# Placing the gate's sum, the transposes of queries and keys, and the last steps of a filler tile in a one-core hybrid attention layer

## The chip, the cores and the metric

The kernel runs on one core of a Trainium2 chip, in fp32 accuracy. The metric is the device time of one execution in microseconds (us). Before the change three runs gave 1677.49, 1675.11 and 1676.13 us; the median is 1676.13 us. A difference of about 0.2% is what the measurement of this kernel can tell from none.

## The reference, cut to what matters

One layer (D = 1024, 1024 latent tokens, 256 context tokens) computes a gated linear attention (GLA, 4 heads) and a differential attention (8 heads) on the same normalised input, and merges them.

```python
for layer in range(DEPTH):                      # DEPTH = 1
    mod_x = silu(c) @ w_ada + b_ada             # shift, scale, gate g_x
    ...
    pl = project(modulate(x, sh_x, sc_x), w_in)
    pc = project(modulate(ctx, sh_c, sc_c), w_in)
    ...
    o_gla = bidir_gla(q, k, v, la_f, la_b, s_f, s_b)
    ...                                         # q1, q2, k1, k2: rms_norm * gain, rotary positions
    o_diff = diff_attention(q1, q2, [ck1, k1], [ck2, k2], [cv, dv], lam)
    # a = softmax(q1 k1 / 8) - lam * softmax(q2 k2 / 8), then a @ v
    a = rms_norm(o_gla) * gla_gain * silu(gla_gate)
    b = rms_norm(o_diff) * diff_gain * (1 - lam_init) * silu(diff_gate)
    y = sigmoid(m_gla) * (a @ w_br_gla) + sigmoid(m_diff) * (b @ w_br_diff)
    x = x + g_x * (y @ w_out)
```

## The kernel before, in words

**Arithmetic.** An fp32 product is made of three TensorE (PE) matmuls per step of 128 rows (`mm3`: high·high, low·high, high·low), because each operand is held as a high and a low part. The splitting is done on ScalarE (ACT), VectorE (DVE) and GpSimd (POOL).

**Who sets the order.** The program is not written in the order in which it runs. Some dozens of Python generators each describe a job. `Driver.run` (L159) keeps a modelled time for every engine, takes the due generator with the lowest priority number, lets it issue instructions up to its next `yield`, and so writes one fixed list for every engine; the chip then only follows semaphores. The modelled time `now` is that of PE: a PE instruction is written at `now`, whether its operands are there on the chip or not. `yield At(t)` comes back up to 1 us before t (`AHEAD`), `yield AtPE(t)` not before PE's time has reached t. So `yield AtPE(e)` says "place what follows on PE where its operand `e` is ready by the model, and not earlier". If the model is too hopeful, PE waits on the chip.

**Stages.** (1) From 0 to about 500 us: the modulation, the normalised input, the projections, `job_gate`. (2) To about 910 us: GLA, interleaved with the projections of dk, dq and m. (3) About 910 to 1466 us: the differential attention. (4) To the end: the output products on PE.

**`job_gate` (L745)** makes the gate g_x: for each half `n`, DVE adds eight scaled rows of weights into `gb` (L764), PE sums over the partitions with a matmul of `ones` and `gb` into the PSUM tile `tp` (L773), and DVE adds the bias. L770 places the matmul.

**`post_qk` (up to L1363)** finishes one tile `p` of queries or keys: squares on ACT, gains, rotary products and sums on DVE, then on POOL the power of -1/2 and its product with the tile (L1343 to L1346); then PE transposes it in four pieces into `tp` (L1353), and it is split and stored. L1347 places the transposes. There are 36 such groups of four.

**Attention.** A unit is one head and 128 queries (64 units); two units make a pair. `att_scores` (L1784) computes for each unit two maps ("components") of 1280 scores in the PSUM tile `s5` (rows `s<-hk,aq`): eight matmuls of 512 columns and four of 256. DVE takes the maxima (`sm<-s`), ACT the exponentials (`e<-s,sm`), which free the bank for the next scores; DVE mixes both maps (`e<-e,sm,e`). `att_tr` (L1877) transposes the mixed map in groups of 4, 4 and 2 (L1897, rows `b<-ident,e`), each group is split (`att_split`: ACT's copy `ac<-b` with POOL's `at<-ac,at`, or ACT and DVE for the third group), and `att_av` (L1902) multiplies the pair with the values: 30 matmuls of 256 columns (rows `b<-at,vv`). `att_fin` follows with two transposes per unit (`b<-ident,b1k`). All these share two PSUM banks, `b1`.

**Filler.** `fill` has the lowest priority and gives PE independent matmuls: half tiles of 8 steps of 3 matmuls (rows `mb<-h,wt`, 128x512) in one PSUM bank, `mb`. 12 tiles are for the m gates (kind 0: eviction by ACT, `ft<-mb`), 8 for the GLA branch (kind 1) and 8 for the other branch (kind 2). A kind 1 tile also loads its gate values. `half_tile` (L2070) comes back to the planner after every step of three, so that a tile can lie open across several scores, transposes and products; the next can begin only when the bank is evicted. What is not filled by the end of stage 3 is done at its end, in other banks.

Of the kernel before, what the change touches and what calls it, by code (L numbers as in the profile page):

```python
# [25 lines left out]
NK = D // P  # L26
# [202 lines left out]
class Hybrid:  # L229
# [515 lines left out]
    def job_gate(self):  # L745


        a = self.a
        yield from self.acq("gb")
        gb = self.t("gb", [P, 2, 512])  # L750
        for n in range(2):
            o = 2048 + n * 512
            for kk in range(NK // 2):
                yield from self.acq("raw")
                raw = self.t("raw", [P, 2, 512])
                self.dma(raw, a["w_ada"][0][kk * 256:(kk + 1) * 256, o:o + 512].rearrange("(k p) c -> p k c", p=P))
                yield self.d.when(raw)
                for j in range(2):
                    k = 2 * kk + j
                    c = self.col[:, k:k + 1]  # L760
                    if k == 0:
                        e = self.dve.tensor_scalar(gb[:, n], raw[:, j], c, None, ALU.mult)
                    else:
                        e = self.dve.scalar_tensor_tensor(gb[:, n], raw[:, j], c, gb[:, n], ALU.mult, ALU.add)  # L764
                    yield e
                self.rel("raw", e)
            yield from self.acq("p")
            bias = self.t("p", [P, 512])
            self.dma(bias, a["b_ada"][0:1, o:o + 512].to_broadcast([P, 512]))
            yield self.d.whenpe(gb)  # L770
            yield from self.acq("tp")
            pm = self.t("tp", [P, 512])
            e = self.mm(pm, self.ones, gb[:, n], True, True)  # L773
            yield e
            yield self.d.when(bias)
            e = self.dve.tensor_tensor(bias, pm, bias, ALU.add)
            self.rel("tp", e)
            yield e
            self.rel("p", self.pool.tensor_scalar(gb[:, n], bias, 0.5, 0.0, ALU.mult, ALU.add))
        self.store([(self.d_gb, gb)], ("gb", 1), ev=self.ev_gb)  # L780
# [531 lines left out]
    def post_qk(self, isk, c, i, pm):  # L1312

        nc = self.nc
        g8 = lambda ap: ap.unsqueeze(1).to_broadcast([P, 8, 64])
        pv = pm.rearrange("p (g e) -> p g e", e=64)
        if isk and (c, i) == (1, 9):
            self.rel("hc", self.d.now, 16)
        yield self.ev_rope[isk]
        yield from self.acq("p", 2)  # L1320
        sq = self.t("p", [P, 8, 64])
        self.act.activation(sq, pv, AF.Square)
        ss = self.t("sm", [P, 8])
        r = self.t("p", [P, 8, 64])
        if i >= 8:
            e = self.dve.tensor_tensor(r, pv, g8(self.gains[:, isk, 0]), ALU.mult)
        else:
            e = self.dve.tensor_tensor(r, pv, g8(self.rope[:, 0, i]), ALU.mult)
        yield self.d.when(sq)
        self.dve.tensor_reduce(ss, sq, AX.X, ALU.add)  # L1330
        if i < 8:
            rv = sq.rearrange("p g (a h e) -> p g a h e", a=2, h=2)
            xv = pv.rearrange("p g (a h e) -> p g a h e", a=2, h=2)
            sv = self.rope[:, 1, i].rearrange("p (a h e) -> p a h e", a=2, h=2)
            for hh in range(2):
                e = self.dve.tensor_tensor(rv[:, :, :, hh], xv[:, :, :, 1 - hh],
                                           sv[:, :, hh].unsqueeze(1).to_broadcast([P, 8, 2, 16]), ALU.mult)
            self.dve.tensor_tensor(r, r, sq, ALU.add)
            if (c, i) == (1, 7):
                self.rel("rope", self.d.when(r))  # L1340
        self.rel("mm", e)
        yield self.d.when(ss)
        self.pool.tensor_scalar(ss, ss, 1.0 / 64, EPS, ALU.mult, ALU.add)  # L1343
        self.pool.tensor_tensor(ss, ss, self.nhalf, ALU.pow)
        yield self.d.when(r)
        e = self.pool.tensor_tensor(r, r, ss.unsqueeze(2).to_broadcast([P, 8, 64]), ALU.mult)  # L1346
        yield AtPE(e)  # L1347
        yield from self.acq("tp")
        yield from self.acq("pl", 2)
        pt = self.t("tp", [P, 4, P])  # L1350
        rf = r.rearrange("p g e -> p (g e)")
        for j in range(4):
            e = self.tr(pt[:, j], rf[:, j * P:(j + 1) * P])  # L1353
        self.rel("p", e, 2)
        yield e
        hi = self.t("pl", [P, 4, P], F32R)
        lo = self.t("pl", [P, 4, P], F32R)
        e = yield from self.split(pt, hi, lo)
        self.rel("tp", e)
        o = self.tok(i) if isk else i * P  # L1360
        dst = [self.d_kT[j][c] if isk else self.d_qT[c][:, :, j] for j in range(2)]
        self.store([(dst[j][:, :, o:o + P].rearrange("h p t -> p h t"), x) for j, x in enumerate((hi, lo))],
                   ("pl", 2), ev=self.ev_st["dk" if isk else "dq", c, i])  # L1363
# [420 lines left out]
    def att_scores(self):  # L1784
# [4 lines left out]
        for hd in range(8):  # L1789
            for qt in range(8):  # L1790
                pr, qs = qt // 2, slice((qt % 2) * P, (qt % 2) * P + P)
                yield self.ev_k[hd]
                yield self.ev_q[hd, pr]
                K, Q = self.K[hd], self.Q[hd, pr]

                def score(po, comp, o, n):
                    bank = po.offset % (2 * T) // 512
                    for j in range(2):
                        e = self.mm(po, Q[comp][:, j, qs], K[comp][:, o:o + n], j == 0, j == 1)
                        self.banked(self.ins, "PE", bank)  # L1800
                    return e

                u = dict(hd=hd, qt=qt, E=[None, None], mt=self.t("sm", [P, 2]), mx=[self.t("sm", [P, 1]) for _ in range(2)],
                         z=self.t("sm", [P, 2]), left=2, ev=[Event() for _ in range(3)])

                for comp in range(2):
                    yield from self.acq(f"s{comp}")
                    pm = s5[:, 1536 * comp:1536 * comp + 1024]
                    for x, (o, n) in enumerate(self.MAIN[comp]):
                        e = score(pm[:, x * 512:(x + 1) * 512], comp, o, n)  # L1810
                        if x == 0:
                            yield AtPE(0)
                    d.spawn(self.att_max(u["ev"][comp], u["mx"][comp], pm, 3 * comp, 3 * comp + 1), On(e, "DVE"), prio=-3)
                    yield AtPE(0)
                    if comp == 0:
                        yield from self.acq("st")
                        pt = s5[:, 1024:1536].rearrange("p (c k) -> p c k", c=2)
                        for x in range(2):
                            e = score(pt[:, x], x, *self.TAIL[x])
                        d.spawn(self.att_max(u["ev"][2], u["mt"], pt, 2), On(e, "DVE"), prio=-3)  # L1820
                    elif qt == 7:
                        self.rel("kk", e, 2)
                    d.spawn(self.att_exp(u, comp, s5), On(e, "DVE"), prio=-3)
                    yield AtPE(0)
                if qt % 2 == 1:
                    self.rel("aq", e, 2)
                d.set(self.ev_u[8 * hd + qt])
# [49 lines left out]
    def att_tr(self):  # L1877

        d = self.d
        for hd in range(8):  # L1880
            for qt in range(8):
# [5 lines left out]
                for g, (k0, n) in enumerate(self.GROUPS):  # L1887
# [5 lines left out]
                    tb = "mc" if "psC" in self.pools else "b1"  # L1893
                    yield from self.acq(tb)
                    pt = self.t(tb, [P, n, P])
                    for j in range(n):
                        e = self.tr(pt[:, j], E[:, (k0 + j) * P:(k0 + j + 1) * P])  # L1897
                    d.spawn(self.att_split(g, pt, hi[:, :, x], lo[:, :, x], self.ev_aT[hd, qt, g], tb), On(e, "ACT"), prio=self.PS)
# [3 lines left out]
    def att_av(self):  # L1902
        d = self.d
        for hd in range(8):
            for pr in range(4):
# [8 lines left out]
                for g, (k0, n) in enumerate(self.GROUPS):  # L1914
                    hi, lo, tg = A[g]
                    for x in range(2):
                        yield self.ev_aT[hd, 2 * pr + x, g]
                    for j in range(n):
                        kt = k0 + j
                        e = self.mm3(po, VH[:, kt], VL[:, kt], hi[:, j].rearrange("p x t -> p (x t)"),  # L1920
# [10 lines left out]
    DT = (0, 4, 1, 5, 2, 6, 3, 7)  # L1931
    PO, FI = "b1", "mb"
    PACE = 1.3
    PT, PA = 1, 2
    PC = ()

# [82 lines left out]
    def fill(self):  # L2019
# [50 lines left out]
        def half_tile(n, half, rhs):  # L2070
# [10 lines left out]
                self.dma(mt, self.d_m[0][s][:, half * 512:(half + 1) * 512])  # L2081
            elif kind == 2:
                d.spawn(self.load_y(s, half), prio=-1)
            for k in range(NK):
                if kind:
                    yield rhs.ev[k, half]
                e = self.mm3(pm, hi[:, k], lo[:, k], rhs[0][k][half], rhs[1][k][half], k == 0, k == NK - 1)
                yield AtPE(0)
            if half == 1:
                self.rel("wt", e, 2)  # L2090
            if kind == 2:
                d.spawn(self.post_y(tg, s, half, pm), e, prio=-1)
            else:
                d.spawn(post(tg, kind, s, half, pm, mt), e, prio=self.PP)
            return e

        class Rhs(list):
            pass
# [396 lines left out]
```

## Time and profile before

| | |
|---|---|
| runs | 1677.49, 1675.11, 1676.13 us |
| profiled execution | 1676.87 us |
| its span, first to last instruction | 1675.2 us |
| mean granted TensorE clock | 0.998 |
| PE busy | 1634.8 us (98%) |
| DVE busy | 1166.3 us (70%) |
| ACT busy | 796.3 us (48%) |
| POOL busy | 606.4 us (36%) |
| PE busy in attention (910 to 1466 us) | 541.0 of 556 us |

How to read it: a matmul's busy time runs from its start to its modelled end, and neighbours overlap; so the start-to-start distance of matmuls, and not the mean busy time of one, tells what a matmul costs. In a timeline row the bracket at the end gives the idle time of the engine just before it and the instruction that ended it; `x12` means that twelve instructions of a kind were merged to a row. In a window row the columns after the stretch are its length, then the busy time and count of PE, PE's weight loads, DVE, ACT and POOL, the granted TensorE clock, the DMA share and GB/s. In a group row stand the busy time and the mean of one, then the idle time just before its members and who ended it.

### The profile page before, as it was taken

What the parts mean: (1) busy time and instruction counts of PE and PEld (TensorE: products, weight loads), DVE (VectorE), ACT (ScalarE), POOL (GpSimd) and SP (SyncE); (2) the same over time, 40 slices, a digit from 0 to 9 for tenths busy, and PEclk for the clock granted to TensorE, in tenths of its full rate; (3) what the DMA queues carried; (4) which work ended last, traced back from release to release, by engine and by line L of the source; (5) the groups of instructions that cost most, each with busy time, mean ns of one, the idle gap of its engine ahead of it and who ended that gap; (6) DMA issues with size and microseconds to landing.
All of it is one profiled execution on the core that took longest, in us unless ns stands there. A gap on an engine that the chain in (4) does not pass through costs nothing.

```text
span 1675.2 us, 24268 instructions
## 1 busy us (share of the span) xinstructions
PE 1634.8 (98%) x8389; PEld 1354.1 (81%) x8389; DVE 1166.3 (70%) x2019; ACT 796.3 (48%) x1640; POOL 606.4 (36%) x649
## 2 busy tenths in 40 slices
PE   7999999999999999999999999999999999999999
PEld 3688788888788888888878887888888888888887
DVE  4797853455578697687762878877887787438594
ACT  4766423343434535455441666665666556413141
POOL 1500200000156575464540544546565565700000
PEclk9999999999999999999999999999999999999999
DMA  8557947677573675646466244334336743277422
GB/s 304 175 204 259 326 163 248 230 276 276 201 251 120 187 218 174 186 137 177 123 187 162 68 122 129 106 107 133 114 107 196 247 126 108 65 255 250 158 78 76
DMA packets 248971, 294.44 MB, mean 176 GB/s; under 512 B 20712, under 2 KB 169104, under 8 KB 248848
## 3 DMA queue, kind: packets, MB, share of 16 engines
q1 hardware_dynamic: 248848, 292.90, 55.4%
q8 instruction: 66, 1.08, 0.3%
q14 instruction: 57, 0.47, 0.1%
HBM read 199.51 MB, written 93.32 MB: 175 GB/s over the span
## 4 chain that ended last, share of the span: by engine, by line
PE 43%; DVE 7%; ACT 3%; issue 2%; POOL 1%; DMA 1%; SPq 0%; ACTq 0%; DVEq 0%; POOLq 0%
PE mc L335 11%; PE mm L335 7%; PE mb L335 7%; PE s L335 6%; PE b L335 5%; DVE sm L197 4%; PE b L361 3%; ACT e L197 2%; DVE e L197 2%; PE go L335 1%; POOL at L197 1%; PE mz L335 1%; PE gs L335 1%; PE tp L361 1%; PE gt L335 1%
## 5 line engine op out<-in xcount | busy, mean ns | idle before, releaser
L335 PE MATMUL mm<-w,h 128*128 128x512 f32 x1260 | 319.1, 402 | 0.6 <-DVE w L197 0.4
L335 PEld LDWEIGHTS mm<-w,h 128*128 128x128 f32 x1260 | 231.9, 189 | 47.9 <-issue 1.0
L197 DVE TENSOR_REDUCE sm<-s 128x1 f32<-128x1024 f32 (+1 forms) x192 | 194.1, 1038 | 44.5 <-PE s L335 38.8
L335 PE MATMUL mb<-h,wt 128*128 128x512 f32 x744 | 202.0, 404 | 0.8 <-ACT ft L197 0.5
L197 ACT ACTIVATE e<-s,sm 128x1280 f32<-128x1280 f32 x128 | 170.1, 1333 | 60.8 <-DVE sm L197 50.0
L197 POOL TENSOR_TENSOR at<-ac,at 128x512 fp32r<-128x512 f32 x128 | 191.2, 1493 | 10.7
L197 POOL TENSOR_SCALAR at<-ac 128x512 fp32r<-128x512 f32 x128 | 101.3, 791 | 251.4 <-ACT ac L197 153.7
L335 PE MATMUL s<-hk,aq 128*128 128x512 f32 (+1 forms) x768 | 179.5, 366 | 6.1 <-ACT e L197 4.2
L335 PEld LDWEIGHTS mb<-h,wt 128*128 128x128 f32 x744 | 130.9, 189 | 24.4 <-ACT ft L197 2.2
L335 PEld LDWEIGHTS s<-hk,aq 128*128 128x128 f32 x768 | 120.5, 189 | 27.2 <-ACT e L197 11.7
L335 PE MATMUL mm<-h,w 128*128 128x512 f32 x576 | 137.6, 394 | 2.2 <-DVE h L197 1.1
L335 PE MATMUL mc<-h,wt 128*128 128x512 f32 x600 | 137.7, 390 | 0.0
L335 PE MATMUL b<-at,vv 128*128 128x256 f32 x960 | 131.3, 285 | 0.5 <-POOL at L197 0.3
L335 PEld LDWEIGHTS mc<-h,wt 128*128 128x128 f32 x600 | 112.1, 188 | 23.1
L335 PEld LDWEIGHTS mm<-h,w 128*128 128x128 f32 x576 | 106.9, 188 | 26.2 <-DVE h L197 1.6
L335 PEld LDWEIGHTS b<-at,vv 128*128 128x128 f32 x960 | 123.3, 190 | 5.7 <-POOL at L197 0.9
L197 DVE TENSOR_TENSOR w<-raw,w 128x512 fp32r<-128x512 f32 x120 | 92.6, 790 | 32.1 <-ACT w L197 30.9
L197 ACT ACTIVATE ac<-b 128x512 f32<-128x512 f32 x120 | 71.1, 601 | 90.9 <-PE b L361 84.2
L197 POOL TENSOR_TENSOR sm<-sm,nhalf 128x2 f32<-128x2 f32 (+2 forms) x94 | 102.3, 1089 | 26.0 <-DVE sm L197 20.8
L197 DVE SCALAR_TENSOR_TENSOR e<-e,sm,e 128x1280 f32<-128x1280 f32 x64 | 110.4, 1725 | 1.0
L197 ACT ACTIVATE w<-raw 128x512 fp32r<-128x512 f32 x120 | 72.5, 629 | 70.8 <-DVE raw L197 22.8
L197 POOL TENSOR_TENSOR p<-p,gdif 128x512 f32<-128x512 f32 x12 | 16.2, 1359 | 242.6 <-DMA d_dv<-pl 194.6
(283 smaller groups left out, 2914.2 us busy)
## 6 DMA issues: line engine op xcount, KB each, us to landing
raw<-in_w_in SPq DMA_DIRECT2D x63, 512.0 KB, 4.5
g<-d_s SPq DMA_DIRECT2D x32, 640.0 KB, 5.0
aq<-d_qT SPq DMA_DIRECT2D x128, 128.0 KB, 3.1
d_dv<-pl SPq DMA_DIRECT2D x40, 256.0 KB, 2.1
gv<-d_v SPq DMA_DIRECT2D x40, 256.0 KB, 3.1
d_kT<-pl SPq DMA_DIRECT2D x40, 256.0 KB, 2.9
hk<-d_kT SPq DMA_DIRECT2D x32, 320.0 KB, 4.9
vv<-d_dv SPq DMA_DIRECT2D x16, 640.0 KB, 5.7
```

Of the source, the lines that this page charges most:

```text
L197: self.ins = f(out, *args, **kw).ins
L335: self.ins = self.nc.tensor.matmul(out, lhsT, rhs, start=start, stop=stop, skip_group_check=more).ins
L361: self.nc.tensor.transpose(out, src, self.ident[:n, :n])
```

## The change

Three places move. The sums on each engine stay the same: 8077 PE instructions in the program, 2021 on DVE, 1408 on ACT, 654 on POOL and 962 on SP, before and now.

1. The gate's sum is placed 4 us of modelled time after `gb` is ready (it was 0).
2. The transposes of a query or key tile are placed 1.5 us after POOL's product is ready (it was 0).
3. A half tile of the filler that is open has its remaining steps written at once ("flushed") at three places, if there are few: one remaining step before the scores of each component, one before each group of transposes, and up to two (`FN`) before the first of the three groups of the values' products (`FG = (0,)`). Steps of kinds 1 and 2 are flushed only if their operands have landed by the model.

```diff
@@ job_gate
-            yield self.d.whenpe(gb)
+            yield AtPE(self.d.when(gb) + 4)
             yield from self.acq("tp")
             pm = self.t("tp", [P, 512])
             e = self.mm(pm, self.ones, gb[:, n], True, True)
@@ post_qk
         e = self.pool.tensor_tensor(r, r, ss.unsqueeze(2).to_broadcast([P, 8, 64]), ALU.mult)
-        yield AtPE(e)
+        yield AtPE(e + 1.5)
@@ att_scores
                     pm = s5[:, 1536 * comp:1536 * comp + 1024]
+                    if self.flush:
+                        self.flush(1)
                     for x, (o, n) in enumerate(self.MAIN[comp]):
@@ att_tr
                     pt = self.t(tb, [P, n, P])
+                    if self.flush:
+                        self.flush(1)
                     for j in range(n):
@@ att_av
                         yield self.ev_aT[hd, 2 * pr + x, g]
+                    if g in self.FG and self.flush:
+                        self.flush(self.FN)
                     for j in range(n):
@@ class
+    flush, FG, FN = None, (0,), 2
@@ half_tile
-            for k in range(NK):
-                if kind:
-                    yield rhs.ev[k, half]
-                e = self.mm3(pm, hi[:, k], lo[:, k], rhs[0][k][half], rhs[1][k][half], k == 0, k == NK - 1)
-                yield AtPE(0)
-            if half == 1:
-                self.rel("wt", e, 2)
-            if kind == 2:
-                d.spawn(self.post_y(tg, s, half, pm), e, prio=-1)
-            else:
-                d.spawn(post(tg, kind, s, half, pm, mt), e, prio=self.PP)
-            return e
+            x = [0, None]
+
+            def step():
+                k = x[0]
+                x[0] += 1
+                e = x[1] = self.mm3(pm, hi[:, k], lo[:, k], rhs[0][k][half], rhs[1][k][half], k == 0, k == NK - 1)
+                if k == NK - 1:
+                    self.flush = None
+                    if half == 1:
+                        self.rel("wt", e, 2)
+                    if kind == 2:
+                        d.spawn(self.post_y(tg, s, half, pm), e, prio=-1)
+                    else:
+                        d.spawn(post(tg, kind, s, half, pm, mt), e, prio=self.PP)
+
+            def flush(n):
+                if 0 < NK - x[0] <= n and not (kind and any(rhs.ev[k, half].t is None or rhs.ev[k, half].t > d.now for k in range(x[0], NK))):
+                    while x[0] < NK:
+                        step()
+
+            self.flush = flush
+            while x[0] < NK:
+                if kind:
+                    yield rhs.ev[x[0], half]
+                if x[0] < NK:
+                    step()
+                    yield AtPE(0)
+            return x[1]
```

**What moves on PE at the second gate sum.** In the rows, `mm` is a projection's PSUM tile, `w` its weights, `h` the activations, `tp` the sum's tile; numbers are buffers. Before, PE in the projections ahead of about 197 us:

```order
L335 MATMUL mm_1961<-w_1385,h_170_720 128x512
L335 MATMUL mm_1961<-w_1384,h_171_721 128x512
L335 MATMUL mm_1961<-w_1639,h_178_763 128x512
L335 MATMUL mm_1961<-w_1640,h_178_763 128x512
L335 MATMUL mm_1961<-w_1639,h_179_764 128x512
L335 MATMUL tp_1973<-gb_1135,ones 128x512
```

And now, at the same sum:

```order
L335 MATMUL mm_2015<-w_1384,h_171_721 128x512
L335 MATMUL mm_2014<-w_1635,h_178_763 128x512
L335 MATMUL mm_2014<-w_1636,h_178_763 128x512
L335 MATMUL mm_2014<-w_1635,h_179_764 128x512
L335 MATMUL tp_2034<-gb_1135,ones 128x512
L335 MATMUL mm_2015<-w_1635,h_178_763 128x512
```

The sum was PE's row 780 and is its row 807: 27 matmuls of 512 columns later; two projection tiles now run side by side around it. (The first sum goes from row 596 to row 611.)

**What moves on PE at the last but one transposes of queries.** `go` and `gs` are GLA's outputs and scores. Before:

```order
L335 MATMUL gs_8187<-gqr_8044,gkk_805_4255 128x64 x2
L335 MATMUL mm_8127<-h_140_598,w_8121 128x512
L335 MATMUL mm_8127<-h_141_599,w_8121 128x512
L335 MATMUL mm_8127<-h_140_598,w_8122 128x512
L361 MATMUL tp_8212<-ident,p_8131 128x128 x4
L335 MATMUL mm_8127<-h_146_613,w_8152 128x512
```

And now:

```order
L335 MATMUL mm_8145<-h_134_577,w_8017 128x512
L335 MATMUL go_8179<-gsf_7803,gqe_7906 128x256
L335 MATMUL go_8179<-gsb_7281,gqe_7909 128x256
L335 MATMUL go_8179<-gv_1569_7806,gsc_8141 128x256
L335 MATMUL go_8179<-gsf_7967,gqe_7906 128x256
L335 MATMUL go_8179<-gsb_7100,gqe_7909 128x256
L335 MATMUL go_8179<-gv_1569_7806,gsc_8141 128x256
L361 MATMUL tp_8186<-ident,p_8077 128x128 x4
L335 MATMUL mm_8145<-h_140_598,w_8052 128x512
```

Six steps of the next tile and GLA's six output matmuls, which stood behind the transposes, now stand ahead of them.

**What moves in a pair of units in the middle of the attention.** `s_1691_8515` is the tile of the scores, `b_...` a bank of transposes, `mb` the filler's bank. Before, PE between two groups of transposes of one map:

```order
L361 MATMUL b_2336_11437<-ident,e_2235_10986 128x128 x4
L335 MATMUL s_1691_8515<-hk_8182,aq_11157 128x512 x4
L335 MATMUL mb_11425<-h_181_766,wt_10679 128x512
L335 MATMUL mb_11425<-h_182_767,wt_10679 128x512
L335 MATMUL mb_11425<-h_181_766,wt_10680 128x512
L335 MATMUL s_1691_8515<-hk_8182,aq_11157 128x256 x2
L335 MATMUL s_1691_8515<-hk_8182,aq_11160 128x256 x2
L335 MATMUL s_1691_8515<-hk_8182,aq_11160 128x512 x4
L361 MATMUL b_2345_11476<-ident,e_2235_10986 128x128 x4
```

And now, at the same place:

```order
L361 MATMUL b_2334_11451<-ident,e_2252_11069 128x128 x4
L335 MATMUL mb_11422<-h_181_766,wt_10807 128x512
L335 MATMUL mb_11422<-h_182_767,wt_10807 128x512
L335 MATMUL mb_11422<-h_181_766,wt_10808 128x512
L335 MATMUL mb_11422<-h_187_792,wt_10807 128x512
L335 MATMUL mb_11422<-h_188_793,wt_10807 128x512
L335 MATMUL mb_11422<-h_187_792,wt_10808 128x512
L361 MATMUL b_2339_11480<-ident,e_2252_11069 128x128 x4
```

The twelve scores that lay between them have moved ahead of the first group, and two steps of the filler stand in their place. ACT's rows there, before (`ac` is the copy of a group of transposes, `e` an exponential):

```order
L197 ACTIVATE e_2328_11419,sm_11284<-s_1691_8515,sm_11282 128x1280
L197 ACTIVATE e_2330_11424,sm_11284<-s_1691_8515,sm_11283 128x1280
L197 ACTIVATE ac_11444<-b_2336_11437 128x512
L197 ACTIVATE b1k_11454,sm_11455<-b_2329_11421 128x128 x2
L197 ACTIVATE ac_11481<-b_2345_11476 128x512
```

And now:

```order
L197 ACTIVATE ac_11456<-b_2334_11451 128x512
L197 ACTIVATE e_2338_11478,sm_11340<-s_1691_8515,sm_11338 128x1280
L197 ACTIVATE ac_11498<-b_2339_11480 128x512
L197 ACTIVATE e_2340_11487,sm_11340<-s_1691_8515,sm_11339 128x1280
L197 ACTIVATE at_2324_11414<-b_2342_11500 128x2x128
```

Two exponentials that stood next to each other now have a copy between them and one ahead of them. From unit 14 to unit 50 every pair of units now takes exactly one half tile of the filler, in four portions of six matmuls, between its transposes.

## The prediction

> **What bounds the kernel now.** I read the page first: busy shares and the chain that ended last.
>
> ```profile
> span 1675.2 us, 24268 instructions
> ...
> PE 1634.8 (98%) x8389; PEld 1354.1 (81%) x8389; DVE 1166.3 (70%) x2019; ACT 796.3 (48%) x1640; POOL 606.4 (36%) x649
> ...
> PE 43%; DVE 7%; ACT 3%; issue 2%; POOL 1%; DMA 1%; SPq 0%; ACTq 0%; DVEq 0%; POOLq 0%
> ```
>
> PE is busy in 98% of the span and carries most of the chain; the change adds and removes no PE work. So it can only gain where PE idles, or runs at a lower clock after idling. At most 1675.2 - 1634.8 = 40.4 us of idle time is there in all. The windows by stage tell where:
>
> ```profile
> 165.00:200.00 35.00, 32.13 (x133) 25.13 (x132) 31.06 (x42) 19.91 (x27) 8.73 (x5) 0.95 0.89 312
> ...
> 500.00:864.00 364.00, 361.95 (x1864) 305.61 (x1862) 284.18 (x530) 178.64 (x487) 208.42 (x260) 1.00 0.57 167
> 864.00:869.00 5.00, 4.25 (x14) 3.51 (x15) 2.27 (x4) 0.60 (x1) 3.94 (x4) 0.66 1.00 252
> ...
> 910.00:1008.00 98.00, 95.00 (x544) 79.90 (x544) 79.37 (x142) 58.90 (x112) 44.85 (x41) 1.00 0.36 100
> 1008.00:1312.00 304.00, 296.41 (x1781) 252.50 (x1782) 242.35 (x458) 184.84 (x380) 174.72 (x158) 1.00 0.46 130
> 1312.00:1466.00 154.00, 149.59 (x940) 129.59 (x939) 110.62 (x221) 84.42 (x183) 95.58 (x88) 1.00 0.42 128
> ```
>
> The second number is PE's busy time. The attention (the last three) idles 3.00 + 7.59 + 4.41 = 15.0 us; the stage before it, 2.05 us in 364. Two short stretches have a low clock (0.95 and 0.66). The waits of PE over the whole span name the causes (total, times, longest):
>
> ```profile
> PE s L335 <- ACT e L197: 4.2, 9, 1.2
> PE b L361 <- DVE at L197: 3.5, 6, 0.9
> PE tp L335 <- DVE gb L197: 2.5, 1, 2.5
> ...
> PE tp L361 <- POOL p L197: 2.2, 1, 2.2
> ...
> PE b L361 <- ACT b1k L197: 1.7, 6, 0.4
> PE b L361 <- ACT ac L197: 1.5, 2, 0.8
> PE b L361 <- DVE b1k L197: 1.3, 4, 0.6
> ...
> PE mm L335 <- DVE w L197: 0.8, 3, 0.4
> ...
> PE mb L335 <- ACT ft L197: 0.5, 2, 0.3
> ```
>
> The third and fourth row are the two single waits that the first two edits touch; the rows of `b` and `s` are the many small ones of the attention.
>
> **Edit 1, the gate's sum.** The timeline of PE around it, then the window of the low clock:
>
> ```profile
> 185.78 8.32 PE L335 MATMUL mm<-w,h 128*128 128x512 f32 x36
> 196.60 2.08 PE L335 MATMUL tp<-gb,ones 128*128 128x512 f32 x2 [2.50 <-DVE gb L197]
> ```
>
> ```profile
> 196.25:199.66 3.41, 3.06 (x5) 1.83 (x6) 3.31 (x5) 2.34 (x4) 1.70 (x1) 0.50 0.91 275
> ```
>
> PE waited 2.50 us for DVE's last `gb`, and then ran 3.41 us at a granted clock of 0.50: the 3.06 us in which it was busy there would have been 1.53 at full clock. Together 2.50 + 1.53 = 4.03 us. The changed order puts 27 matmuls of 512 columns ahead of the sum. The distance of one, from a stretch in which PE never waits, is 137.7 / 600 = 0.23 us:
>
> ```profile
> L335 PE MATMUL mc<-h,wt 128*128 128x512 f32 x600 | 137.7, 390 | 0.0
> ```
>
> 27 x 0.23 = 6.2 us, more than the wait of 2.50. The sum itself costs PE the same as before; its result goes to DVE and POOL and is stored for the last stage, so nobody waits for it behind, and no DMA is moved ahead of a load that is due. Late next would be the weights of the projections: over the whole span PE waited 0.8 us in three pieces for DVE's `w` (row above). Bounds: a gain of 0 (the weights come no earlier) to 4.03. I take **4.0**, nearest to the rows.
>
> The Trainium skill ("TensorE: Matmul & The Clock Gate", section "🎯 Why this matters for your kernels") wants no idle gaps over about 3 us between bursts, since the clock drops after them. The trace halves it after a gap of 2.50 us, so the measurement decides. By the page this gap and the next would cost no clock, and the two edits would be worth 2.50 + 2.24 = 4.7 us.
>
> **Edit 2, the transposes of queries and keys.** 36 groups move, and one of them waited. The timeline of PE, POOL and DVE there:
>
> ```profile
> 855.32 0.85 PE L335 MATMUL mm<-h,w 128*128 128x512 f32 x3
> ...
> 859.86 1.89 PE L335 MATMUL gs<-gqr,gkk 128*128 128x64 f32 x16
> ...
> 861.56 0.94 PE L335 MATMUL mm<-h,w 128*128 128x512 f32 x3
> ...
> 863.65 1.04 POOL L197 TENSOR_TENSOR p<-p,sm 128x512 f32<-128x512 f32 x1
> 863.94 1.30 DVE L197 TENSOR_TENSOR w<-raw,w 128x512 fp32r<-128x512 f32 x1
> ...
> 864.75 0.67 PE L361 MATMUL tp<-ident,p 128*128 128x128 f32 x4 [2.24 <-POOL p L197]
> ...
> 868.87 0.59 PE L335 MATMUL go<-gsf,gqe 128*128 128x256 f32 x2
> ...
> 870.16 0.60 PE L361 MATMUL tp<-ident,p 128*128 128x128 f32 x4
> ```
>
> ```profile
> 865.26:868.67 3.41, 3.41 (x11) 2.69 (x10) 1.01 (x2) 0.60 (x1) 2.77 (x3) 0.50 0.95 244
> ```
>
> The tile's projection ended at about 855.3; POOL's product ended at 864.69, 9.4 us later. PE had only 862.5 - 855.3 = 7.2 us of work in between, waited 2.24, and then did 3.41 us of work at clock 0.50, which is 1.7 more than at full clock: 3.9 together. In the changed order 42 matmuls of 512 columns, the 16 small ones (859.86 to 861.56, 1.70 us) and six of `go` (868.87 to 870.16, 1.29) lie there: 42 x 0.23 + 1.70 + 1.29 = 12.6 us, 3.2 more than the chain takes. The other 35 groups did not wait before and are placed later, so they cannot wait more for POOL. What is moved with them is each group's split on ACT and DVE and its two stores on SP. The last group stood 910.12 - 870.16 = 40 us ahead of the first scores (row below) and now stands 144 large matmuls and 4 us of small ones ahead, 37 us; the queries' loads behind its stores took 3.1 us to land, so they stay hidden.
>
> ```profile
> 910.12 2.13 PE L335 MATMUL s<-hk,aq 128*128 128x512 f32 x10 [0.74 <-ACT p L197]
> ```
>
> ```profile
> aq<-d_qT SPq DMA_DIRECT2D x128, 128.0 KB, 3.1
> ```
>
> The cover has a weak point: DVE's conversion `w` above ran until 865.24, half a microsecond past the end of the wait, so the next weights were hidden behind it. Bounds 0 to 3.9; I take **3.9**, since the changed order gives PE six steps of another tile there.
>
> **Edit 3, the flush.** Its gain can't be over the idle 15.0 us of the attention. What it does is to make the filler regular: from unit 14 to 50 six fill matmuls (6 x 0.23 = 1.38 us) lie between one group of transposes and the next. The transposes' waits, 3.5 + 1.7 + 1.5 + 1.3 = 8.0 us, had a longest piece of 0.9 us, so 1.38 us more work covers them; 36 of 64 units give 8.0 x 36 / 64 = 4.5 us. Of the 3.5 us that stand for the other 28 units I take half, 1.8, since the flush works there too, but not in every pair. The 4.2 us for ACT's exponentials I leave where they are, since these now have copies between them (below). Against it: with more filler done by unit 48 than before, it runs dry at units 50 to 53, where the next half tile waits for its operands; the longest waits of such small kinds were 1.2 and 0.9, and two of some 0.75 make -1.5. The sum is 4.5 + 1.8 - 1.5 = **4.8**, nearer to the transposes' rows than to the whole idle time. Bounds: 15.0 above, and below zero the price of the last rival.
>
> What speaks for caution is DVE and ACT in the middle window:
>
> ```profile
> L197 DVE TENSOR_REDUCE sm<-s 128x1 f32<-128x1024 f32 x72 | 87.6, 1216 | 9.1 <-PE s L335 4.3 <-ACT e L197 3.1 <-ACT ft L197 1.2
> ```
>
> ```profile
> L197 ACT ACTIVATE e<-s,sm 128x1280 f32<-128x1280 f32 x73 | 97.0, 1334 | 29.4 <-DVE sm L197 20.2 <-PE b L361 3.5 <-DVE e L197 3.5
> L197 ACT ACTIVATE ac<-b 128x512 f32<-128x512 f32 x70 | 41.8, 602 | 57.9 <-PE b L361 54.6 <-POOL at L197 2.6 <-POOL sm L197 0.6
> ```
>
> 36 units (72 maxima) took 304 us, so 16.9 us a pair, and DVE was busy 242.35 / 18 = 13.5 of it. PE without any idle time would need 296.41 / 18 = 16.5. PE stays the fuller engine, but DVE at 80% feeds ACT and ACT feeds PE, and a chain through three such engines seldom runs without waits.
>
> **Sum.** 4.0 + 3.9 + 4.8 = 12.7 us. The profiled execution took 1676.87 us, 0.7 above the median 1676.13; 1676.87 - 12.7 = 1664.2, and with the 0.7 taken off **1663.4** for a median.
>
> **The rivals.**
>
> *The attention gives nothing.* The waits move from the transposes to the scores, because DVE and ACT pace the pair. For it: DVE's 80%, and 20.2 us in which ACT's exponentials waited for DVE's maxima. Against it: DVE needs 13.5 of 16.9 us. The time: 1676.1 - 7.9 = 1668.2.
>
> *An early stall comes back as another.* PE arrives 4 us earlier at weights that DVE converts when it can; above all at edit 2, where the conversion ended at 865.24. For it: that row. Against it: only 0.8 us of waits for `w` in the span. With edit 2 lost: 1676.1 - (12.7 - 3.9) = 1667.3.
>
> *The whole does nothing.* Both early stalls come back and the attention stays: 1676.1. The rows of PE make it unlikely, as the sums above have 3 us to spare.
>
> *Slower: the exponential stands behind a copy.* ACT's changed order has an `ac` copy ahead of each of two exponentials of a pair, and each copy waits for transposes that PE reaches only after six fill matmuls. The next scores wait for the exponential. If ACT has no slack at that place, each pair gets 2 x 0.602 = 1.2 us longer, 18 x 1.2 = 21.7 us in the regular part; with the other terms 1676.1 - 12.7 + 21.7 = 1685.1. It decides from 12.7 / 18 = 0.71 us a pair on. For it: the 4.2 us for `e` are the largest wait already. Against it: ACT was busy only 184.84 of 304 us.
>
> **How the numbers follow.** The forecast (all three pay, attention from +1 to +12) has 0.52; nothing from the attention 0.22; an early stall back 0.12; no effect 0.06; slower 0.08. The likeliest gives 1663.4. The range goes up to 1672 for the second and third case with 4 to 5 us of doubt in the attention, and down to 1655 for an attention that gives 13 of its 15 us; it leaves out the last two cases and a few hundredths at its ends. A measurement of this kernel tells about 0.2%, 3.4 us, from no change. Faster by more: 0.52 + 0.22 + 0.12 less 0.02 = 0.84; within it 0.06 + 0.02 = 0.08; slower 0.08.
>
> **What would show it.** Edit 1: no wait of `tp` for `gb`, and a granted clock of 1.00 from 190 to 200 us. Edit 2: no wait of `tp` for POOL's `p` of over 0.5 us, and no wait for `w` in its place. Edit 3: PE's idle time in the attention falls from 15.0 to about 10 us, mostly in the waits of `b` for `at`, `ac` and `b1k`; a wait of `mb` late in the attention. The forecast is wrong if the waits of `s` for `e` grow beyond 10 us, or if a new stall of over 2 us, with its 3.4 us at half clock, appears in the GLA stage, whose order the planner wrote anew.

## The result, and the profile after

The changed kernel takes 1653.84 us (median of four runs, 1653.11 to 1654.77), against 1675.62 us before in the same comparison (1672.31 to 1677.49): a ratio of 0.987, with a 95% interval of 0.9855 to 0.9885. It is 21.8 us faster; the forecast was 12.7 us, 1663.4 us, and its range ended at 1655. Its profiled execution has a span of 1652.1 us.

The page of the changed kernel, with the same parts as quoted of before:

```profile
span 1652.1 us, 24253 instructions
...
PE 1627.2 (98%) x8389; PEld 1355.0 (82%) x8389; DVE 1162.3 (70%) x2019; ACT 798.9 (48%) x1640; POOL 595.4 (36%) x649
...
PE 88%; DVE 5%; DMA 3%; ACT 2%; issue 1%; POOL 0%; SPq 0%; DVEq 0%; ACTq 0%
```

PE is busy for 98% in both, though the span is 23 us shorter. So that share doesn't tell what was to be had; the chain does a little (PE's part went from 43% to 88%).

The first two edits, on PE's timeline of the changed kernel, with the window in which the clock had been halved:

```profile
201.64 1.02 PE L335 MATMUL tp<-gb,ones 128*128 128x512 f32 x2
```

```profile
196.60:199.66 3.06, 3.06 (x15) 2.52 (x15) 2.77 (x5) 0.00 (x0) 0.60 (x1) 1.00 0.89 283
```

```profile
852.07 0.50 PE L335 MATMUL mm<-h,w 128*128 128x512 f32 x1 [0.49 <-DVE w L197]
...
861.16 0.60 PE L361 MATMUL tp<-ident,p 128*128 128x128 f32 x4
```

The sum and the transposes have no bracket any more, the clock is 1.00, and one wait of 0.49 us for weights is new. The first scores start at 902.41 us; they started at 910.12: 7.7 us earlier.

The attention in three stretches, units 0 to 14, 14 to 50, and from 50 to the last product with the values. First the kernel before, then the changed one:

```profile
910.12:1008.35 98.23, 95.00 (x545) 79.91 (x545) 79.72 (x142) 59.18 (x113) 44.85 (x41) 1.00 0.36 101
1008.35:1312.51 304.16, 296.91 (x1784) 252.88 (x1785) 242.51 (x458) 184.49 (x378) 174.72 (x158) 1.00 0.46 130
1312.51:1467.39 154.88, 150.47 (x950) 130.59 (x949) 110.27 (x221) 84.81 (x184) 95.58 (x88) 1.00 0.42 130
```

```profile
902.41:1003.46 101.05, 98.96 (x570) 84.59 (x571) 82.35 (x148) 61.11 (x117) 46.80 (x42) 1.00 0.39 106
1003.46:1301.21 297.75, 297.75 (x1837) 257.90 (x1836) 248.93 (x459) 190.44 (x388) 171.04 (x163) 1.00 0.53 147
1301.21:1447.00 145.79, 141.64 (x881) 123.24 (x880) 107.57 (x214) 79.79 (x172) 87.20 (x83) 0.99 0.37 109
```

In the middle stretch PE is busy all of the 297.75 us. Idle time in the whole attention fell from 14.9 to 6.2 us, by 8.7. But the time fell by more. A better measure is the **loss**: the length of a stretch less the work in it, where each PE instruction of the program's order counts with its start-to-start distance in a full stream (0.227 us for 512 columns, 0.120 for 256, 0.109 for a transpose):

```
loss in us      units 0-14   14-50   50-end   attention
before              6.8       18.3      9.2      34.2
changed             3.9        5.1      9.7      18.8
```

That is 15.4 us less, with the 7.7 us ahead of the first scores 23.1 us, which is the difference of the spans, 1675.2 - 1652.1. Not all of a loss is waiting: of the 5.1 us left in units 14 to 50, only 1.3 us lie in distances that are over 0.1 us longer than in the full stream; the rest are smaller pieces. Why idle time shows less than the loss, a timeline of PE before shows, at the end of a half tile of the filler, and then ACT there:

```profile
1024.81 0.60 PE L361 MATMUL b<-ident,e 128*128 128x128 f32 x4
1026.17 0.88 PE L361 MATMUL b<-ident,e 128*128 128x128 f32 x6 [0.77 <-ACT ac L197]
1026.81 0.94 PE L335 MATMUL mb<-h,wt 128*128 128x512 f32 x3
```

```profile
1025.52 0.60 ACT L197 ACTIVATE ac<-b 128x512 f32<-128x512 f32 x1 [0.28 <-PE b L361]
1026.02 0.59 ACT L197 ACTIVATE ft<-mb 128x512 f32<-128x512 f32 x1
```

Four transposes are worth 0.44 us and the next came 1.36 us after them: 0.93 us lost. The bracket says 0.77, because the modelled end of the last transpose reaches into the gap. A wait that such a modelled end covers whole, here up to 0.16 us, leaves no idle time at all.

PE's waits over the whole span of the changed kernel:

```profile
PE s L335 <- ACT e L197: 4.5, 4, 1.9
...
PE b L335 <- ACT ac L197: 0.8, 1, 0.8
...
PE b L361 <- ACT ac L197: 0.3, 1, 0.3
...
PE b L361 <- DVE b1k L197: 0.2, 1, 0.2
```

The waits of transposes in `b` went from 8.0 to 0.5 us; those of scores for exponentials were 4.2 and are 4.5 us, but none of them lies in units 14 to 50.

### The profile page after: what moved, and what is told of

The parts are those of the page before. It is cut to its first block, busy times and chain, and to the rows that moved or that the text cites. A ratio compares the mean times of both kernels' runs of the same rounds, so it can differ in the third digit from the quotient of the medians.

```text
span 1652.1 us, 24253 instructions
## 1 busy us (share of the span) xinstructions
PE 1627.2 (98%) x8389; PEld 1355.0 (82%) x8389; DVE 1162.3 (70%) x2019; ACT 798.9 (48%) x1640; POOL 595.4 (36%) x649
## 4 chain that ended last, share of the span: by engine, by line
PE 88%; DVE 5%; DMA 3%; ACT 2%; issue 1%; POOL 0%; SPq 0%; DVEq 0%; ACTq 0%
PE mm L335 31%; PE mc L335 11%; PE mb L335 9%; PE s L335 8%; PE b L335 6%; PE tp L335 5%; PE b L361 4%; PE go L335 4%; PE gs L335 4%; PE gt L335 4%; DVE sm L197 2%; PE tp L361 2%; DMA raw<-in_w_in 1%; PE mz L335 1%; ACT e L197 1%
## 5 line engine op out<-in xcount | busy, mean ns | idle before, releaser
L335 PE MATMUL s<-hk,aq 128*128 128x512 f32 (+1 forms) x768 | 176.1, 364 | 5.2 <-ACT e L197 4.5
L197 POOL TENSOR_TENSOR at<-ac,at 128x512 fp32r<-128x512 f32 x128 | 173.4, 1355 | 10.7
L197 POOL TENSOR_TENSOR sm<-sm,nhalf 128x2 f32<-128x2 f32 (+2 forms) x94 | 114.5, 1218 | 14.2 <-DVE sm L197 8.8
L197 DVE SCALAR_TENSOR_TENSOR e<-e,sm,e 128x1280 f32<-128x1280 f32 x64 | 116.8, 1824 | 1.5
L197 DVE TENSOR_TENSOR w<-raw,w 128x512 fp32r<-128x512 f32 x120 | 85.8, 737 | 30.7 <-ACT w L197 29.7
```

Source lines behind the costliest of these rows:

```text
L197: self.ins = f(out, *args, **kw).ins
L335: self.ins = self.nc.tensor.matmul(out, lhsT, rhs, start=start, stop=stop, skip_group_check=more).ins
```

## The experiments

All twelve were timed beside the kernel before, whose median was 1674.9 to 1675.7 us in the three comparisons. "Loss" is the attention's, as above.

**One early edit alone.**

```diff
 # gate alone: post_qk as before, no call of flush
-        yield AtPE(e + 1.5)
+        yield AtPE(e)
```

> Only the gate's sum placed 4 us later. By the terms of the prediction: 4.0 us faster than before, 1671.6, no wait of tp for gb, first scores at about 906.1 us instead of 910.1. Rival (PE arrives earlier at weights that are not there): 0 to 2 us faster. The attention's order is written anew by this small shift, so its waits may move the total by 3 us either way; the start of the first scores is the cleaner number.

1670.53 us, ratio 0.997 (0.9958 to 0.9983): 4.4 us faster. The gate's wait is gone, and the transposes of queries wait as before:

```profile
861.30 1.12 PE L361 MATMUL tp<-ident,p 128*128 128x128 f32 x4 [2.23 <-POOL p L197]
```

First scores at 907.85 us, 2.3 earlier, where 906.1 was expected; in this execution the clock was at half for 6.83 us around that wait (from 860.38 us on) and not for 3.41. The other part of the gain is a loss of 31.8 in the attention in place of 34.2, whose order the small shift has renewed.

```diff
 # transposes alone: job_gate as before, no call of flush
-            yield AtPE(self.d.when(gb) + 4)
+            yield self.d.whenpe(gb)
```

> Only the transposes of queries and keys placed 1.5 us later. By the terms of the prediction: 3.9 us faster, 1671.7, first scores at about 906.2 us. Rival (the wait comes back at the weights converted on DVE): 0 to 1.5 us faster, with a wait of mm for w of about 1 to 2 us near 860 us.

1669.69 us, ratio 0.9965 (0.995 to 0.998): 5.2 us faster, 2.7 of which again stand in the attention's order (loss 31.5, nearly as with the gate alone). First scores came at 908.32 us, only 1.8 earlier, where 906.2 was expected. But the first gate sum, up to which the order on PE is that of before, already came 2.4 us later in this execution (153.5 and not 151.1 us), so about 4.2 us were gained behind it. The weights took 0.49 us in place of the 2.24, so the rival has a fifth of it.

**Both early edits, no flush.**

```diff
-                    if self.flush:
-                        self.flush(1)
...
-                    if g in self.FG and self.flush:
-                        self.flush(self.FN)
```

> Both early edits, no flush. By the terms: 7.9 us faster, 1667.7, first scores at 902.4 us as in the changed kernel. If the attention gains only by the flush, its length stays within 3 us of before's 556 us. Rival (any new order of the attention would have done it): the total is at 1660 or lower.

1667.03 us, ratio 0.9946 (0.9927 to 0.9964): 7.9 us faster. First scores at 902.04 us, 8.1 earlier, loss 31.5. So both stalls are gone and do not come back as others; but 2.7 of the 7.9 us are again the smaller loss in the attention, which neither term contains. The flush is worth 1667.0 - 1653.8 = 13.2 us on top of both.

**The flush alone** (both early edits undone).

> Only the flush. If the flush alone makes the attention's gain: about 15 us faster, 1660.5, with no wait of PE from unit 14 to 50 and first scores at about 910 us. By the term of the prediction: 4.8 us, 1670.8. Rival (the flush needs the early edits): between 1665 and 1672.

1660.14 us, ratio 0.9903 (0.9886 to 0.9919): 14.8 us faster, first scores at 910.97 us, loss 18.1. The flush needs nothing of the other two, and is worth three times my term.

**Which of the three places.** My reason was that the order becomes regular, with filler between groups of transposes (theory A). The rival was that each flush pays for itself, by freeing the filler's bank (theory B).

```diff
 # no flush before the transposes
                     pt = self.t(tb, [P, n, P])
-                    if self.flush:
-                        self.flush(1)
```

> The changed kernel without the flush before the transposes; it is left before the scores and the values' products. Theory A (what pays is that the order falls into one repeated pair from unit 14 on, in which work covers every wait): the same time as the changed kernel, 1654 within 2 us, since this order repeats the very same pair 17 times. Theory B (each flush pays for itself, by freeing the filler's bank earlier): 3 to 6 us slower than the changed kernel.

1658.33 us, ratio 0.9893 (0.9876 to 0.9909). The repeated pair from unit 14 to 50 is the same, and so is its loss, 5.2; all of the 4.5 us lies behind unit 50 (14.1 in place of 9.7). The number fits B and not A; the place does not settle it.

```diff
 # no flush before the values' products
-                    if g in self.FG and self.flush:
-                        self.flush(self.FN)
```

> The changed kernel without the flush before the values' products. The order has 17 different pairs among 18. Theory A: most of the attention's gain is lost, 1663 to 1668. Theory B: about a third of it is lost, 1658 to 1660.

1666.35 us, ratio 0.9943 (0.9928 to 0.9958), loss 32.5. The flushes before scores and transposes alone gain nothing over none (1667.0). B, as a gain for each flush, is refuted with that; the number is A's.

```diff
                     if self.flush:
-                        self.flush(1)
+                        self.flush(2)
                     for x, (o, n) in enumerate(self.MAIN[comp]):
```

> The changed kernel with up to two steps flushed before the scores instead of one: more flushing, but an order with 18 different pairs among 18. Theory A: most of the attention's gain is lost, 1663 to 1668. Theory B: as the changed kernel or faster, 1650 to 1655.

1653.48 us, ratio 0.9866 (0.9851 to 0.988). No two pairs of this order are alike, and it is as fast as the changed kernel; its loss is 18.8 as well (2.7, 12.0 and 4.1 in the three stretches). A is refuted for the whole: the gain doesn't need a repeated pair. In units 14 to 50 alone it is not, for there the repeated pair loses 5.1 us and this order 12.0; it makes up for that at both ends.

```diff
 # no flush; both early edits
-    PM, PS, PF, PP = -2, -3, -2, -1
+    PM, PS, PF, PP = -3, -3, -2, -1
```

(The constant that was changed is `PM`, the priority of the mixing in `att_mix`; the expectation names `att_fin` wrongly.)

> No flush; both early edits; and att_fin placed by priority -3 instead of -2, which alone makes the order repeat one pair (and a variant of it) from unit 18 to 44, with 24 filler matmuls in each, in portions of 6, 9, 6 and 3, and two groups of transposes back to back. Theory A: hardly a wait in units 20 to 44, under 0.2 us a pair, total 1656 to 1661. Theory B: waits there as in the kernel before, 0.4 us a pair or more, total 1664 to 1668. Theory C (it is the filler between every two groups of transposes that pays): waits of about 0.5 us a pair at the second group.

1677.42 us, ratio 1.0014 (1.0004 to 1.0023), loss 43.3. This order repeats itself and is the slowest of all but one: what it repeats is a wait, as PE's waits in units 14 to 50 say.

```profile
PE b L361 <- DVE at L197: 7.4, 14, 2.8
```

So a repeated order alone does not bring the gain. It is no clean test of more than that, since the edit also puts DVE's mixing ahead, and the waits are for DVE's `at`. None of the three theories gave this time: it is the first group of transposes that waits there, once in most pairs, and not the second.

**A new theory, D.** With one bank, the filler is *closed* from the last matmul of a half tile until ACT has evicted it and the next one starts. I counted these stretches in the traces, from unit 14 to 50, and the waits that lie in them (distances of starts over 0.1 us longer than in the full stream):

```
                    stretches   us each        us in all   PE's waits, and of them while closed
before                 17        0.9 to 9.0       99         14.4      11.6
no flush               16        0.9 to 11.8      71         12.0       7.5
changed                17        8.1 to 8.3      139          1.3       1.3
```

In the kernel before, 11.6 of 14.4 us of the waits lie in the 99 of 304 us in which the filler is closed. In a short stretch PE waits for the eviction itself, behind whatever ACT has to do first (above: `ft` starts only when the copy of the transposes is done, and PE has nothing else). A long one has groups of transposes in it, with nothing to put between them. In the changed kernel the filler is closed for longer, 139 of 298 us, and PE hardly waits: every closed stretch holds the values' products and scores. (The kernel without the flush also has 4.5 us of waits while the filler is open; they are gone too, and D gives no reason for those.) PE's timeline of one of the changed kernel's stretches:

```profile
1051.65 1.64 PE L335 MATMUL mb<-h,wt 128*128 128x512 f32 x6
1053.13 0.62 PE L335 MATMUL s<-hk,aq 128*128 128x512 f32 x2
1053.59 0.38 PE L361 MATMUL b<-ident,b1k 128*128 128x128 f32 x2
1053.72 2.11 PE L335 MATMUL s<-hk,aq 128*128 128x512 f32 x10
1055.67 0.60 PE L361 MATMUL b<-ident,e 128*128 128x128 f32 x4
1056.02 2.40 PE L335 MATMUL b<-at,vv 128*128 128x256 f32 x18
1058.26 0.60 PE L361 MATMUL b<-ident,e 128*128 128x128 f32 x4
1058.61 1.68 PE L335 MATMUL b<-at,vv 128*128 128x256 f32 x12
1060.13 1.09 PE L335 MATMUL s<-hk,aq 128*128 128x512 f32 x4
...
1061.19 1.65 PE L335 MATMUL mb<-h,wt 128*128 128x512 f32 x6
```

```profile
1054.28 0.59 ACT L197 ACTIVATE ft<-mb 128x512 f32<-128x512 f32 x1
```

The half tile ends at 1053.1, is evicted by 1054.9, and the next starts at 1061.19, with 6 us to spare; the two groups of transposes in between have 18 and 12 products behind them. D says: the flush before the values' products pays since it closes the bank where PE has 30 products and the scores to do. Three experiments test it.

```diff
 # flush only before the values' products
-                    if self.flush:
-                        self.flush(1)
                     for x, (o, n) in enumerate(self.MAIN[comp]):
...
-                    if self.flush:
-                        self.flush(1)
                     for j in range(n):
```

> The changed kernel with the flush only before the first group of the values' products. The kernel without that one lost the whole gain of the flush (1666.4 against 1667.0 with no flush at all), so theory D says: what pays is that the filler's bank is closed while PE has 30 values' products and the scores to do, and this flush does it; then 1654 to 1659. If it needs the flush before the scores as well (theory E, only the two together put the end of a half tile in one place of the pair): 1661 to 1667.

1657.68 us, ratio 0.9897 (0.988 to 0.9913), loss 22.1. This one place has 9.3 of the 13.2 us. The order has no repeated pair.

```diff
 # in the changed kernel
+                for _ in range(2):
+                    self.act.eng.activation(mt, pm, AF.Tanh, scale=0.5)
                 self.rel(tg, self.act.activation(mt, pm, AF.Tanh, scale=0.5))
```

> The changed kernel with the eviction of each of the 24 gate half tiles done three times over on ACT (the two added ones write the same values and are not counted by the planner, so that the order on PE and all else stays as it is): the filler's bank is closed for 1.2 us more each time. Theory D: in the changed kernel the bank is closed for 8.1 us or more between half tiles, with other work for PE, so this costs 0 to 3 us, 1654 to 1657. Rival (ACT's own time is what counts): 8 us or more slower, as the next one.

1656.51 us, ratio 0.989 (0.9875 to 0.9905): 2.7 us slower than the changed kernel. From unit 14 to 50 it costs nothing (loss 5.1, as without it); what it costs lies in the first 14 units (loss 7.3 in place of 3.9), ahead of the repeated pair. PE waits 1.5 us for the eviction there and 1.3 us for POOL's `at`, and the changed kernel has neither.

The same edit in the kernel with both early edits and no flush:

> The same two added evictions in the kernel without the flush (both early edits in it, 1667.0 us). Theory D: there 6 of 16 closed stretches from unit 14 to 50 are under 3 us, and PE waits while the bank is closed; so some 9 of 24 pay 1.2 us in full: 8 to 14 us slower, 1675 to 1681. Rival (ACT's own time): the same loss as in the kernel with the flush.

1679.23 us, ratio 1.002 (1.0011 to 1.003): 12.2 us slower than without it (1667.03), 8.2 of which lie in units 14 to 50 (loss 23.9 in place of 15.7). The windows of units 14 to 50, first with the flush, then without:

```profile
1009.62:1307.35 297.73, 297.73 (x1837) 257.88 (x1836) 248.44 (x459) 211.50 (x424) 170.88 (x163) 1.00 0.52 145
```

```profile
1001.62:1306.59 304.97, 291.96 (x1785) 249.49 (x1784) 237.88 (x457) 203.11 (x411) 171.98 (x162) 1.00 0.46 127
```

ACT was busier with the flush (211.50 us) than without (203.11), and PE still never idled; so it is not ACT's load as such but what PE has to do while the bank is closed. Without the flush PE's waits for the eviction come up in the same window:

```profile
PE mb L335 <- ACT ft L197: 4.3, 5, 1.7
```

They were 0.5 us without the added evictions. By the count above, all that the evictions add lies in closed stretches: 16.6 of 20.2 us of waits, in place of 7.5 of 12.0. But not all of the added waiting is for `ft`: PE's waits for ACT's exponentials, copies and `b1k` went from 1.9 to 4.2 us, and those the added evictions may have held up directly. No run tells the two apart.

**What is left, and a faster version.** In the changed kernel the loss behind unit 50 did not fall. PE's timeline there, and DVE's, which evicts the half tiles of kind 1:

```profile
1312.00 0.60 PE L361 MATMUL b<-ident,e 128*128 128x128 f32 x4
1314.49 1.73 PE L335 MATMUL s<-hk,aq 128*128 128x512 f32 x4 [1.89 <-ACT e L197]
```

```profile
1317.46 0.68 DVE L197 SCALAR_TENSOR_TENSOR ft<-ft,mb 128x512 f32<-128x512 f32 x1
```

The first half tile of kind 1 ended at 1301.2 and was evicted at 1317.46: closed for 17 us.

```diff
-                        d.spawn(post(tg, kind, s, half, pm, mt), e, prio=self.PP)
+                        d.spawn(post(tg, kind, s, half, pm, mt), e, prio=-4 if kind else self.PP)
```

> The changed kernel with the eviction of a GLA-branch half tile (kind 1) at priority -4 on DVE instead of -1. In the changed kernel the filler stops for a whole pair at unit 50, and the order has no filler matmul between units 50 and 52; here it has 15 there. If the waits of units 50 to 52 (5 us over the pitch) come from the bank that DVE evicts late, the time is 1649 to 1652; if they come from something else there, 1653 to 1655.

1648.60 us, ratio 0.9845 (0.9829 to 0.9861): 5.2 us faster than the changed kernel, and the fastest version here. The eviction is at 1308.34, and the loss behind unit 50 is 4.4 in place of 9.7.

The losses of the attention and the times go together: for the ten kernels with both early edits (the changed one and nine variants) the time less the loss lies between 1633.9 and 1635.6 us, over losses from 13.6 to 43.7.

## Why the prediction was wrong

- **The gate, 4.0 us:** right in its mechanism: the wait and the half clock are gone. 4.4 us with this edit alone, but 2.4 of them in the attention's loss.
- **The transposes of queries and keys, 3.9 us:** right in the same way. The weak point that I named, the conversion of `w`, cost 0.49 us.
- **Both together:** the time fell by 7.9 us (forecast 7.9) and the first scores came 8.1 us earlier. That the time agrees to a tenth is partly luck, since 2.7 of the 7.9 are a smaller loss in the attention that no term contained. The time less the attention's loss was 1641.1 us before (mean of its four medians, less 34.2) and is 1634.9 on the average of the ten kernels with both edits: 6.2 us by that measure.
- **The flush, 4.8 us:** this is the term that failed. It measured 13.2 us on top of the early edits (12.7 of loss) and 14.8 alone (16.1 of loss). Two steps of it were wrong, and one bound.
  - "The transposes' waits, 3.5 + 1.7 + 1.5 + 1.3 = 8.0 us [...] 36 of 64 units give 8.0 x 36 / 64 = 4.5 us": the size was taken from idle time. The transposes' idle waits in units 14 to 50 were 4.1 us, near the 4.5, and all of them went; but the loss there fell by 13.2 us, from 18.3 to 5.1. Over the attention idle time held 8.7 of the 15.4 us; the others are pieces that the modelled ends of matmuls cover.
  - "The 4.2 us for ACT's exponentials I leave where they are": 3.1 of them lay in units 14 to 50, 2.6 while the filler was closed, and they went to nothing with the others.
  - "Its gain can't be over the idle 15.0 us" is no bound, for the same reason: with the flush alone the loss fell by 16.1 us. That the time stayed just below 15.0 doesn't save it. "PE without any idle time would need 296.41 / 18 = 16.5" has the same fault, since the busy time holds covered waits.
- **The reason I gave, six fill matmuls between groups of transposes,** describes the order but is not what pays: an order without a repeated pair is as fast, a repeated order without the flush is slower than before. What the runs show for most of the gain is what PE has to do while the filler's bank is closed; the flush that places this stretch has 9.3 of the 13.2 us alone, and a longer eviction costs nothing in units 14 to 50 with the flush and 8.2 us there without it. It was to be seen in the trace of before, had I asked in what stretches the waits lie and not only which operand ended them.
- **"It runs dry at units 50 to 53 [...] make -1.5":** right in kind. It costs about 5 us (1.89 us of waiting and a halved clock behind it among them), as the version with the earlier eviction shows. The operand awaited was the bank.
- **The signs and the rivals.** None of the named signs of being wrong came up; PE's idle time in the attention fell further than forecast, to 6.2 and not 10 us. None of the rivals happened. For "the exponential stands behind a copy" ACT had slack enough: even with 1.2 us more on ACT in every pair PE did not wait from unit 14 to 50.

The page of the profile has PE at 98% on both sides. The Trainium skill ("Perfetto Trace Analysis", section "Identifying the Most-Contended Engine") says that matmul busy time is a poor measure of how near a kernel is to its limit. The trace agrees: 98% before and 98% after a gain of 21.8 us.

What stays open: the waits that went though the filler was open, and why the flush before the transposes, whose middle part is the same with and without it, is worth 4.5 us behind unit 50. The trace shows where they lie. Without that flush units 58 to 62 lose 7.9 us (1.0 in the changed kernel): a half tile ends at 1369.2 us, and the next starts only at 1392.9. PE waits 2.51 us for an exponential in between, with the clock at half for 3.41 us from 1379.08 us on. The bank was free at 1373.0 us, so here it was not the eviction that kept the filler closed; the new half tile's third matmul waited 1.43 us for its weights on DVE. No run took that place apart.

## What to carry to other kernels

Take what a wait costs from the distance of starts against a full stream, not from idle time: here idle time showed 8.7 of 15.4 us. Filler work in one buffer has a stretch in which it can't fill, between its last step and the end of its eviction; place that stretch where the engine has long work that waits for nothing, and ask of every wait whether the filler was closed just then. An order that repeats itself is no merit by itself: it may repeat a wait.

## What the runs showed of the hardware

The granted clock fell to 0.50 with each of PE's gaps of 2.23 us and more behind the start of the kernel, eight in six of these kernels: at the gate, at the transposes of queries, and in the attention of two experiments. It stayed there for 3.41 us, and once, with the gate alone at the transposes, for 6.83. Gaps of 1.89 to 1.91 us were followed by it in two of four cases. The changed kernel and the one without the flush before the transposes wait 1.89 us at the same place of the same order; the first then ran 3.41 us at half clock, and the second stayed at 1.00. The windows of the kernel with the gate alone, of the changed one, and of the one without the flush before the transposes:

```profile
860.38:867.21 6.83, 5.91 (x16) 4.91 (x17) 2.44 (x4) 0.60 (x1) 4.12 (x4) 0.50 0.95 249
```

```profile
1314.92:1318.33 3.41, 3.07 (x13) 2.27 (x12) 3.17 (x7) 1.15 (x3) 2.76 (x3) 0.50 0.35 110
```

```profile
1315.00:1318.50 3.50, 2.69 (x14) 1.79 (x14) 3.50 (x7) 2.19 (x4) 2.83 (x3) 1.00 0.47 150
```

DVE's mixing of the two maps took longer and POOL's subtraction less in the changed order, at the same shapes (before 1722 and 1523 ns in the window from 1008 to 1312 us). The changed kernel's groups, DVE and POOL, in units 14 to 50:

```profile
L197 DVE SCALAR_TENSOR_TENSOR e<-e,sm,e 128x1280 f32<-128x1280 f32 x36 | 70.0, 1946 | 1.3
```

```profile
L197 POOL TENSOR_TENSOR at<-ac,at 128x512 fp32r<-128x512 f32 x72 | 93.3, 1296 | 6.0
```

The traces show what changed: which of the two starts first when they run side by side. In the changed kernel 18 of the 36 mixings started about 0.3 us after a subtraction; they took 2.34 us on the average and the other 18 took 1.55, while the subtractions took 1.29 beside them. In the kernel before, 14 subtractions started while a mixing ran; they took 2.36 us on the average, and those with no mixing beside them 1.31. So it is mainly the one that starts later that takes longer; no run varied this by itself. Such a pair of the changed kernel, and one of before:

```profile
1024.70 1.29 POOL L197 TENSOR_TENSOR at<-ac,at 128x512 fp32r<-128x512 f32 x1
1025.02 2.31 DVE L197 SCALAR_TENSOR_TENSOR e<-e,sm,e 128x1280 f32<-128x1280 f32 x1
```

```profile
1038.16 1.99 DVE L197 SCALAR_TENSOR_TENSOR e<-e,sm,e 128x1280 f32<-128x1280 f32 x1
1038.90 2.40 POOL L197 TENSOR_TENSOR at<-ac,at 128x512 fp32r<-128x512 f32 x1
```
